# Expert up projections: half of the contraction on fp32r operands in two parts, the other half in plain fp32

## The chip, the cores and the metric

The kernel runs on one core of a Trainium2 chip. The metric is the device time of one execution in microseconds (us): the median of three timed runs. A profile of one further execution shows what each engine did: TensorE (PE, with PEld for its weight loads), VectorE (DVE), ScalarE (ACT), GpSimd (POOL) and SyncE (SP, here only a DMA queue).

## The reference

The program is a two-layer backbone. Each layer normalizes and modulates 512 latent tokens and 256 context tokens of width 1024, mixes them by attention and a gated delta rule, and then runs a mixture of 32 experts. The second layer gives no context output, so its experts see the latent tokens only. The change lies in the experts:

```python
def expert_block(args):
    xi, e = args
    return (jax.nn.silu(xi @ w1[e]) * (xi @ w3[e])) @ w2[e]

y = lax.map(expert_block, (xb, blk_e)).reshape(P, D)
return jax.ops.segment_sum(y[dest] * w_s[:, None].astype(y.dtype), tok_s, num_segments=N)
```

Each token goes to two experts. `w1` and `w3` of an expert are 1024x256 (the up projections), `w2` is 256x1024 (the down projection), all fp32: 1 MB each, 3 MB per expert, 32 experts, two layers.

## The kernel before

One block of up to 128 tokens belongs to each expert. `experts` (L1408) walks over the 32 experts of a layer in a loop that is software pipelined over three experts. In the pass of expert e it

- issues the loads of expert e + 3 (`load`, on SP's queue; `w13` holds w1 and w3 in four buffers, `w2` in three, constants `RB, RB2`),
- multiplies the turned token block `xt` with `w13` into the PSUM tile `pab`, in two groups of four 128-row slices (`expert_up`, L1351), and between the two groups turns the product `u` of expert e - 1 (`expert_turn`: two transposes into `gt`, ScalarE's copy `gh`, VectorE's rest `gl`) and scatters the output of expert e - 2 (`ey` on VectorE, L1400, then a scatter-add `yd` by an indirect DMA from GpSimd's queue, L1405),
- splits `w2` of expert e into two parts (`split`: ScalarE writes `w2h`, L1329, in the type fp32r, VectorE the rest `w2l` = `w2` - `w2h`, L1330),
- makes the gate rows `eg` (`row_gates`: ScalarE, and in layer 0, where latent and context tokens have gates of their own, VectorE too, L1381),
- turns the gathered tokens `xe` of expert e + 1 (`expert_rows`: eight transposes in two groups, each copied by ScalarE to `xt`, L1345),
- computes `u` = silu times the other half (`expert_mid`: ScalarE's tanh and two VectorE instructions, all named `eu`),
- multiplies the turned `u` of expert e - 1 with its `w2` (`expert_down`: twelve products into `py`, L1393), and fetches the tokens of expert e + 4 (gather `xe`, L1334).

In plain fp32 a product appears as two records of TensorE; the down projection uses three fp32r products for each slice, `gh` x `w2h`, `gl` x `w2h` and `gh` x `w2l`, one record each. The order on each engine is that of the program: `pin` (L162) ties each instruction of the stage to the one before it on its engine. The DMAs on SP's queue are not pinned; a scheduler orders them. Each queue issues in order, so a DMA that waits for its buffer holds up those behind it. In some early experts the loop also takes a step of `route_rest`, small instructions on all engines that place overflowing tokens.

Of the kernel before, what the change touches and what calls it, by code (L numbers as in the profile page):

```python
# [13 lines left out]
F32 = mybir.dt.float32  # L14
F32R = mybir.dt.float32r
BF16 = mybir.dt.bfloat16
I32 = mybir.dt.int32
AF = mybir.ActivationFunctionType
OP = mybir.AluOpType
# [4 lines left out]
P = 128  # L24
# [6 lines left out]
NE = 32  # L31
# [63 lines left out]

NOV = 12
NC = NE + NOV
RB, RB2 = 4, 3
YL = 1
XI = 2  # L100
WH = 3
# [42 lines left out]
class Model:  # L144
# [17 lines left out]
    def pin(self, ins):  # L162

        if self.pinned:
            e = ins.ins.engine.name
            if self.last.get(e):
                self.tc.add_manual_dep(ins.ins, self.last[e], mybir.DependencyInfo(mybir.DependencyClass.NoSync, mybir.DependencyReason.DATA), reason="order")
            self.last[e] = ins.ins.name
        return ins
# [1152 lines left out]
        nc.sync.dma_start(dst, src.rearrange("(p k) f -> p k f", **dims))  # L1322
        return w

    def split(self, src, pool, eng):
        nc = self.nc
        hi = pool.tile([P, 2048], F32R, tag="w2h", bufs=2, name="w2h")
        lo = pool.tile([P, 2048], F32R, tag="w2l", bufs=2, name="w2l")
        self.pin(nc.scalar.activation(hi, src, AF.Copy))  # L1329
        self.pin(eng.tensor_tensor(lo, src, hi, op=OP.subtract))  # L1330
        return hi, lo

    def gather(self, idx, xe, h2d, ntok):
# [3 lines left out]
    def expert_rows(self, xe, pool):  # L1337

        nc, pin = self.nc, self.pin
        xt = pool.tile([P, 8, P], F32, tag="xt", bufs=2, name="xt")  # L1340
        for q in range(2):
            ps = self.psC("xt")
            for k in range(4):
                pin(nc.tensor.transpose(ps[:, k * P:(k + 1) * P], xe.rearrange("p (q k) -> p k q", k=8)[:, 4 * q + k, :], self.ident))  # L1344
            pin(nc.scalar.activation(xt[:, 4 * q:4 * q + 4, :], ps.rearrange("p (k n) -> p k n", k=4), AF.Copy))  # L1345
        return xt

    def expert_up(self, pa, xt, w13, ks):

        for k in ks:  # L1350
            self.pin(self.nc.tensor.matmul(pa.rearrange("p (a f) -> p a f", a=2), xt[:, k, :], w13[:, :, k, :], start=(k == 0), stop=(k == 7)))  # L1351

    def expert_mid(self, pa, pool):

# [53 lines left out]
    def experts(self, i, R, js, g5, h2d, yd, ntok, xw):  # L1408


        nc, tc = self.nc, self.tc
        idx, wt = R["idx"], [R[nm] for nm in ("wsl", "wc") if nm in R]
        col = lambda c: idx[:, c:c + 1]
        w13, raw2, w2, x, u, g, gates, py = {}, {}, {}, {}, {}, {}, {}, {}

        def load(e):
            if e < NE:
                for n in range(2):
                    w13[e] = self.expert_load(i, e, n, xw)
                raw2[e] = self.expert_load(i, e, 2, xw)  # L1420

        def fetch(e):
            if e < NE:
                self.gather(col(e), xes[e % XE], h2d, ntok)

        def rows(e):
            if e < NE:
                x[e] = self.expert_rows(xes[e % XE], xp)

        def turn(e):  # L1430
            if e >= 0:
                g[e] = self.expert_turn(u.pop(e), xp)

        def down(e):
            if e >= 0:
                py[e] = self.expert_down(g.pop(e), w2.pop(e))

        def out(e):
            if e >= 0:
                y = self.expert_out(py.pop(e), gates.pop(e), xp)  # L1440
                self.expert_add(y, col(e), yd, ntok)

        self.pins(False)
        for n in range(2):
            w13[0] = self.expert_load(i, 0, n, xw)
        stored = yield
        with tc.issue_after(stored.ins):
            raw2[0] = self.expert_load(i, 0, 2, xw)
            for e in range(1, LA):
                load(e)  # L1450
        xp = yield
        rest = self.route_rest(R, js, xp)
        eo, nb = R["eo"], R["nb"]
        xes = []
        self.pins(True)
        for e in range(XE):
            xes.append(xp.tile([P, D], F32, name="xe%d" % e, tag="xe%d" % e))
            self.pin(nc.gpsimd.memset(xes[e], 0.0))
            fetch(e)
        rows(0)  # L1460
        for e in range(NE):
            load(e + LA)
            pa = self.psA("pab")
            xt, w = x.pop(e), w13.pop(e)
            self.expert_up(pa, xt, w, range(0, 4))
            turn(e - 1)
            out(e - 2)
            self.expert_up(pa, xt, w, range(4, 8))
            w2[e] = self.split(raw2.pop(e), xw, nc.vector)
            gates[e] = self.row_gates([w[:, e:e + 1] for w in wt], g5, xp)  # L1470
            rows(e + 1)
            u[e] = self.expert_mid(pa, xp)
            down(e - 1)
            fetch(e + XE)
            if e >= E0:
                next(rest, None)
        turn(NE - 1)
        out(NE - 2)
        down(NE - 1)
        out(NE - 1)  # L1480
        self.pins(False)
        assert not list(rest)
        n = nc.values_load(nb[0:1, 0:1], min_val=0, max_val=NOV)  # L1483
        with tc.If(n > 0):
            with tc.For_i(0, n, 1) as j:
                ev = nc.values_load(eo[0:1, bass.ds(j, 1)], min_val=0, max_val=NE - 1)
                ic = xp.tile([P, 1], I32, tag="ic", name="ic")
                wo = [xp.tile([P, 1], F32, tag="wo%d" % z, name="wo") for z in range(len(wt))]
                nc.vector.tensor_copy(ic, idx[:, bass.ds(NE + j, 1)])
                for a, w in zip(wo, wt):  # L1490
                    nc.vector.tensor_copy(a, w[:, bass.ds(NE + j, 1)])
                ws = [self.expert_load(i, ev, n, xw) for n in range(3)]
                self.gather(ic, xes[0], h2d, ntok)
                xr = self.expert_rows(xes[0], xp)
                pa = self.psA("pab")
                self.expert_up(pa, xr, ws[0], range(8))
                po = self.expert_down(self.expert_turn(self.expert_mid(pa, xp), xp), self.split(ws[2], xw, nc.vector))
                self.expert_add(self.expert_out(po, self.row_gates(wo, g5, xp), xp), ic, yd, ntok)
        yield

# [268 lines left out]
```

## Time and profile before

| | us |
|---|---|
| median of three timed runs | 2114.71 (2108.64 to 2114.74) |
| profiled execution | 2130.51 |
| its span in the profile | 2128.7 |
| TensorE busy (share of the span) | 1824.3 (86%) |
| VectorE busy | 1272.6 (60%) |
| ScalarE busy | 893.5 (42%) |
| GpSimd busy | 839.5 (39%) |
| fp32 records of the up projection, L1351 | 465.5 |

The profiled execution is one run, 15.8 us over the median of the others. The experts of layer 0 run from about 753 to 1096 us of the span, those of layer 1 from about 1753 to 2095. Busy time of TensorE is pipelined, so its records overlap; the distance between starts tells its pace.

### The profile page before, as it was taken

To read this page: it belongs to the slowest core of one execution; us is meant where nothing else is said; L and a number is where in the kernel's file an instruction comes from. 1 tells how busy PE (TensorE), PEld (TensorE's weight loads), DVE (VectorE), ACT (ScalarE), POOL (GpSimd) and SP (SyncE) were. 2 spreads that over 40 slices of the span, in tenths; PEclk is the share of its full clock that TensorE was granted. 3 is DMA by queue.
4 is the path that set the end of the run, shared out by engine and by line. 5 is a ranking of instruction groups with operands and counts; after the bars stand their busy time and mean duration, and the time that the engine had idled before them with its cause. 6 is when DMAs were issued, how large, how long until landed. Compare 5 with 4: busy or idle time off the path is not lost. (4 is left out here: it accounts for less than half of the span.)

```text
span 2128.7 us, 34974 instructions
## 1 busy us (share of the span) xinstructions
PE 1824.3 (86%) x13579; PEld 1349.2 (63%) x13579; DVE 1272.6 (60%) x2344; ACT 893.5 (42%) x1531; POOL 839.5 (39%) x915
## 2 busy tenths in 40 slices
PE   6998798888868789999978987767888769999995
PEld 4887687666657655565547876656566555566553
DVE  3469996566672645555546689963676443444443
ACT  3444245655541134444425543334464223444442
POOL 4456653244354323223326376520333632223221
PEclk9999897798988889999998988766998779999997
DMA  8222435787655588889924224356862568888872
GB/s 278 72 71 79 127 117 175 233 230 237 199 135 131 198 329 329 323 320 328 331 65 140 80 71 120 107 170 182 252 186 70 174 265 307 326 315 302 314 263 85
DMA packets 227684, 427.77 MB, mean 201 GB/s; under 512 B 83720, under 2 KB 157180, under 8 KB 202939
## 3 DMA queue, kind: packets, MB, share of 16 engines
q1 hardware_dynamic: 171547, 329.09, 45.9%
q0 software_dynamic: 33536, 72.59, 12.1%
q10 hardware_dynamic: 22432, 23.81, 3.3%
q8 instruction: 109, 1.79, 0.3%
q14 instruction: 60, 0.49, 0.1%
HBM read 386.82 MB, written 84.67 MB: 221 GB/s over the span
## 5 line engine op out<-in xcount | busy, mean ns | idle before, releaser
L1351 PE MATMUL pab<-w,xt 128*128 128x512 f32 x1024 | 465.5, 598 | 0.5 <-ACT xt L1345 0.5
L1351 PEld LDWEIGHTS pab<-w,xt 128*128 128x128 f32 x1024 | 189.7, 192 | 191.3 <-issue 186.5
L1405 POOL DMA_INDIRECT yd<-ey,idx x64 | 116.8, 1824 | 472.3 <-DMA yd<-ey,idx 196.9
L1372 DVE TENSOR_TENSOR gl<-gt,gh 128x256 fp32r<-128x256 f32 x64 | 27.1, 424 | 276.1 <-ACT gh L1371 272.5
L1330 DVE TENSOR_TENSOR w2l<-w,w2h 128x2048 fp32r<-128x2048 f32 x64 | 147.4, 2303 | 44.4 <-ACT w2h L1329 43.0
L1371 ACT ACTIVATE gh<-gt 128x256 fp32r<-128x256 f32 x64 | 24.5, 383 | 348.9 <-PE gt L1367 348.9
L238 PE MATMUL pn<-whi,hh 128*128 128x256 f32 (+1 forms) x432 | 133.9, 313 | 15.3 <-ACT gev L1541 11.4
L488 POOL TENSOR_TENSOR wlo<-wraw,whi 128x1024 fp32r<-128x1024 f32 (+1 forms) x44 | 112.0, 2547 | 82.8 <-ACT whi L487 81.9
L238 PE MATMUL po<-woh,m 128*128 128x512 f32 x320 | 113.0, 431 | 27.8 <-ACT woh L1068 20.6
L238 PE MATMUL pn<-whi,hl 128*128 128x256 f32 (+1 forms) x432 | 133.4, 313 | 0.7 <-DVE hl L349 0.4
L238 PE MATMUL pn<-wlo,hh 128*128 128x256 f32 (+1 forms) x432 | 133.0, 309 | 0.6 <-POOL wlo L488 0.6
L238 PE MATMUL pt<-hh,wlo 128*128 128x512 f32 (+1 forms) x352 | 125.4, 356 | 0.0
L238 PE MATMUL pt<-hh,whi 128*128 128x512 f32 (+1 forms) x352 | 124.3, 353 | 0.0
L238 PE MATMUL pt<-hl,whi 128*128 128x512 f32 (+1 forms) x352 | 123.8, 352 | 0.0
L1329 ACT ACTIVATE w2h<-w 128x2048 fp32r<-128x2048 f32 x64 | 121.7, 1902 | 0.0
L1393 PE MATMUL py<-w2h,gh 128*128 128x512 f32 x256 | 107.7, 421 | 4.4 <-DVE ey L1400 4.4
L1345 ACT ACTIVATE xt<-xt 128x512 f32<-128x512 f32 x128 | 69.7, 595 | 86.8 <-PE xt L1344 86.0
L517 DVE SCALAR_TENSOR_TENSOR dT<-xin,cw,dT 128x772 f32<-128x772 f32 x64 | 79.4, 1243 | 42.2 <-ACT dT L515 40.5
L238 PEld LDWEIGHTS pn<-whi,hh 128*128 128x128 f32 x432 | 90.1, 210 | 20.8 <-ACT gev L1541 12.1
L1393 PE MATMUL py<-w2l,gh 128*128 128x512 f32 x256 | 101.6, 397 | 0.0
L1393 PE MATMUL py<-w2h,gl 128*128 128x512 f32 x256 | 101.2, 395 | 0.0
L1344 PEld LDWEIGHTS xt<-cst,xe 128*128 128x128 f32 x512 | 67.9, 192 | 50.2 <-issue 29.8
(391 smaller groups left out, 4561.8 us busy)
## 6 DMA issues: line engine op xcount, KB each, us to landing
w<-w SPq DMA_DIRECT2D x192, 1024.0 KB, 10.0
araw<-ada_w POOLq DMA_DIRECT2D x40, 1024.0 KB, 9.3
wraw<-w_in SPq DMA_DIRECT2D x40, 512.0 KB, 4.1
lk<-vk SPq DMA_DIRECT2D x48, 256.0 KB, 7.2
lx<-xad SPq DMA_DIRECT2D x40, 256.0 KB, 9.3
araw<-ada_w SPq DMA_DIRECT2D x8, 1024.0 KB, 11.8
wr<-w_out SPq DMA_DIRECT2D x8, 1024.0 KB, 15.4
vk<-vr ACTq DMA_DIRECT2D x16, 384.0 KB, 3.2
```

The costliest lines, as they stand in the source:

```text
L238: self.nc.tensor.matmul(ps, a(k), b(k), start=(first and n == 0), stop=(last and n == 3 * nk - 1))
L488: getattr(nc, eng).tensor_tensor(lo, raw, hi, op=OP.subtract)
L517: nc.vector.scalar_tensor_tensor(dst, xin[:, tap:tap + 772], cw[:, tap, f:f + 1], dst, op0=OP.mult, op1=OP.add)
L1329: self.pin(nc.scalar.activation(hi, src, AF.Copy))
L1330: self.pin(eng.tensor_tensor(lo, src, hi, op=OP.subtract))
L1344: pin(nc.tensor.transpose(ps[:, k * P:(k + 1) * P], xe.rearrange("p (q k) -> p k q", k=8)[:, 4 * q + k, :], self.ident))
L1345: pin(nc.scalar.activation(xt[:, 4 * q:4 * q + 4, :], ps.rearrange("p (k n) -> p k n", k=4), AF.Copy))
L1351: self.pin(self.nc.tensor.matmul(pa.rearrange("p (a f) -> p a f", a=2), xt[:, k, :], w13[:, :, k, :], start=(k == 0), stop=(k == 7)))
L1371: pin(nc.scalar.activation(gh, p3, AF.Copy))
L1372: pin(nc.vector.tensor_tensor(gl, p3, gh, op=OP.subtract))
L1393: pin(self.nc.tensor.matmul(py[:, n * 512:(n + 1) * 512], a[:, j, :], b[:, c], start=(j + m == 0), stop=(j == 1 and m == 2)))
L1405: self.pin(self.nc.gpsimd.indirect_dma_start(out=yd, out_offset=bass.IndirectOffsetOnAxis(ap=idx, axis=0), in_=y, in_offset=None, bounds_c ...
```

## The change

The first half of the contraction (four of the eight 128-row slices, constant `KS`) is computed from operands in two parts: three fp32r products in place of one fp32 product. For this `expert_rows` copies the first four turned slices as `xth` (ScalarE) and `xtl` (VectorE, from PSUM minus `xth`), and a new step `parts` splits the first half of `w13` into `w13h` (ScalarE) and `w13l` (VectorE), through the same `split`. The parts of `w13` have one buffer each, those of `w2` two as before. `parts` of expert e + 1 stands in the loop after the second group of `expert_up` and before the split of `w2`. The other half of the contraction stays in fp32. The raw `w2` goes from three buffers to two. The block for overflowing tokens gets the same split.

```diff
-RB, RB2 = 4, 3
+RB, RB2 = 4, 2
+KS = 4
...
-    def split(self, src, pool, eng):
-        nc = self.nc
-        hi = pool.tile([P, 2048], F32R, tag="w2h", bufs=2, name="w2h")
-        lo = pool.tile([P, 2048], F32R, tag="w2l", bufs=2, name="w2l")
+    def split(self, src, name, pool):
+
+        nc = self.nc
+        hi, lo = [pool.tile([P, 2048], F32R, tag="s" + name + z, bufs=2 if name == "w2" else 1, name=name + z) for z in "hl"]
+        if len(src.shape) == 4:
+            hi, lo = [a.rearrange("p (a k f) -> p a k f", a=2, k=KS) for a in (hi, lo)]
         self.pin(nc.scalar.activation(hi, src, AF.Copy))
-        self.pin(eng.tensor_tensor(lo, src, hi, op=OP.subtract))
+        self.pin(nc.vector.tensor_tensor(lo, src, hi, op=OP.subtract))
...
-        xt = pool.tile([P, 8, P], F32, tag="xt", bufs=2, name="xt")
+        xh, xl = [pool.tile([P, KS, P], F32R, tag=nm, bufs=2, name=nm) for nm in ("xth", "xtl")]
+        xt = pool.tile([P, 8 - KS, P], F32, tag="xt", bufs=2, name="xt")
...
-            pin(nc.scalar.activation(xt[:, 4 * q:4 * q + 4, :], ps.rearrange("p (k n) -> p k n", k=4), AF.Copy))
-        return xt
-
-    def expert_up(self, pa, xt, w13, ks):
-
-        for k in ks:
-            self.pin(self.nc.tensor.matmul(pa.rearrange("p (a f) -> p a f", a=2), xt[:, k, :], w13[:, :, k, :], start=(k == 0), stop=(k == 7)))
+            p3 = ps.rearrange("p (k n) -> p k n", k=4)
+            pin(nc.scalar.activation(xt if q else xh, p3, AF.Copy))
+            if q == 0:
+                pin(nc.vector.tensor_tensor(xl, p3, xh, op=OP.subtract))
+        return xh, xl, xt
+
+    def expert_up(self, pa, x, w13, hi_lo, half):
+
+        (xh, xl, xt), (hi, lo) = x, hi_lo
+        out = pa.rearrange("p (a f) -> p a f", a=2)
+        for k in range(4):
+            if half == 0:
+                for m, (a, b) in enumerate(((xh, hi), (xl, hi), (xh, lo))):
+                    self.pin(self.nc.tensor.matmul(out, a[:, k, :], b[:, :, k, :], start=(k + m == 0), stop=False))
+            else:
+                self.pin(self.nc.tensor.matmul(out, xt[:, k, :], w13[:, :, KS + k, :], start=False, stop=(k == 3)))
...
+        def parts(e):
+            if e < NE:
+                p13[e] = self.split(w13[e][:, :, 0:KS, :], "w13", xw)
...
+        parts(0)
         rows(0)
...
-            self.expert_up(pa, xt, w, range(0, 4))
+            self.expert_up(pa, xt, w, hl, 0)
             turn(e - 1)
             out(e - 2)
-            self.expert_up(pa, xt, w, range(4, 8))
-            w2[e] = self.split(raw2.pop(e), xw, nc.vector)
+            self.expert_up(pa, xt, w, hl, 1)
+            parts(e + 1)
+            w2[e] = self.split(raw2.pop(e), "w2", xw)
```

On VectorE, one pass of the loop in layer 0 reads before the change (`w_...` is a raw weight buffer, `eg` the gate row):

```order
L1372 TENSOR_TENSOR gl<-gt,gh 128x256 [waits Activation_49]
L1400 TENSOR_TENSOR ey<-py,eg 128x1024 [waits DMASW4_49]
L1330 TENSOR_TENSOR w2l<-w_8191,w2h 128x2048 [waits DMAHW5_49,Activation_49]
L1381 SCALAR_TENSOR_TENSOR eg<-g_7326,wc,eg 128x1024 [waits Activation_49]
L1358 SCALAR_TENSOR_TENSOR eu<-eu,pab 128x256 [waits PE_49,Activation_49]
L1359 SCALAR_TENSOR_TENSOR eu<-eu,pab 128x256 [waits DVE_49]
```

and after it:

```order
L1385 TENSOR_TENSOR gl<-gt,gh 128x256 [waits Activation_49]
L1413 TENSOR_TENSOR ey<-py,eg 128x1024 [waits DMASW4_49]
L1333 TENSOR_TENSOR w13l<-w_8315,w13h 128x2048 [waits DMAHW3_49,DMAHW2_49,Activation_49]
L1333 TENSOR_TENSOR w2l<-w_8228,w2h 128x2048 [waits DMAHW7_49,Activation_49]
L1394 SCALAR_TENSOR_TENSOR eg<-g_7326,wc,eg 128x1024 [waits Activation_49]
L1352 TENSOR_TENSOR xtl<-xt,xth 128x512 [waits Activation_49]
L1371 SCALAR_TENSOR_TENSOR eu<-eu,pab 128x256 [waits Activation_49]
L1372 SCALAR_TENSOR_TENSOR eu<-eu,pab 128x256 [waits DVE_49]
```

The split of the next expert's up weights stands ahead of that of `w2`, and `xtl` behind both and behind the gate.

On TensorE, the end of one down projection, the first group of the next expert and the turn read after the change (before it, the group was four products `pab<-w,xt` in a row):

```order
L1406 MATMUL py<-w2l,gh 128x512
L1362 MATMUL pab<-w13h,xth 128x512 [waits Activation_49]
L1362 MATMUL pab<-w13h,xtl 128x512 [waits DVE_49]
L1362 MATMUL pab<-w13l,xth 128x512
L1362 MATMUL pab<-w13h,xth 128x512
```

The second product of the group waits for VectorE, and `gt` still follows the group.

On SP's queue, where a name that comes twice in a row is a pair w1 and w3 and a single one is `w2`, the early loads of layer 0 read before the change

```order
L1322 DMA w_8127<-w 128x2048 [waits DMAHW6_49,PE_49]
L1322 DMA w_8127<-w 128x2048 [waits DMAHW7_49]
L1322 DMA w_8188<-w 128x2048 [waits DMAHW0_49,PE_49]
L1322 DMA w_8188<-w 128x2048 [waits DMAHW1_49]
L1322 DMA w_8130<-w 128x2048 [waits DMAHW2_49,DVE_49]
```

and after it

```order
L1323 DMA w_8225<-w 128x2048 [waits DMAHW7_49,PE_49]
L1323 DMA w_8225<-w 128x2048 [waits DMAHW0_49]
L1323 DMA w_8096<-w 128x2048 [waits DMAHW1_49,DVE_49]
L1323 DMA w_8315<-w 128x2048 [waits DMAHW2_49,PE_49]
L1323 DMA w_8315<-w 128x2048 [waits DMAHW3_49]
L1323 DMA w_8152<-w 128x2048 [waits DMAHW6_49,DMAHW4_49,DVE_49]
```

Before, `w_8130` (of expert 4) follows the pair of expert 5; after, `w_8096` (of expert 3) follows it: the load of `w2` stands one expert later against the pairs, and waits for the split that ends the use of its buffer.

## Rows read from the trace of the kernel before

**Rows 1.** Windows: stretch, length, busy us of engines (instructions), granted clock, DMA share, GB/s.

```profile
752.00:774.00 22.00, 21.76 (x68) 11.90 (x67) 9.00 (x9) 9.97 (x13) 1.98 (x2) 0.90 0.84 322
774.00:850.00 76.00, 76.00 (x268) 45.18 (x267) 42.73 (x50) 32.21 (x42) 24.34 (x25) 1.00 0.85 321
```

**Rows 2.** Timeline, TensorE, one expert: start, length, instruction, count [idle before, releaser].

```profile
827.66 3.60 PE L1351 MATMUL pab<-w,xt 128*128 128x512 f32 x8
831.09 0.39 PE L1367 MATMUL gt<-cst,eu 128*128 128x128 f32 x2
...
835.88 0.39 PE L1393 MATMUL py<-w2h,gl 128*128 128x512 f32 x1
...
838.44 3.60 PE L1351 MATMUL pab<-w,xt 128*128 128x512 f32 x8
841.88 0.39 PE L1367 MATMUL gt<-cst,eu 128*128 128x128 f32 x2
```

**Rows 3.** Timeline, VectorE, the same expert of layer 0.

```profile
831.99 0.42 DVE L1372 TENSOR_TENSOR gl<-gt,gh 128x256 fp32r<-128x256 f32 x1 [4.61 <-ACT gh L1371]
832.33 1.21 DVE L1400 TENSOR_TENSOR ey<-py,eg 128x1024 f32<-128x1024 f32 x1
833.79 2.29 DVE L1330 TENSOR_TENSOR w2l<-w,w2h 128x2048 fp32r<-128x2048 f32 x1 [0.25 <-ACT w2h L1329]
836.00 1.28 DVE L1381 SCALAR_TENSOR_TENSOR eg<-g,wc,eg 128x1024 f32<-128x1024 f32 x1
837.20 0.41 DVE L1358 SCALAR_TENSOR_TENSOR eu<-eu,pab 128x256 f32<-128x256 f32 x1
837.64 0.42 DVE L1359 SCALAR_TENSOR_TENSOR eu<-eu,pab 128x256 f32<-128x256 f32 x1
```

**Rows 4.** Timeline, ScalarE, the same expert.

```profile
831.85 1.90 ACT L1329 ACTIVATE w2h<-w 128x2048 fp32r<-128x2048 f32 x1
833.65 1.14 ACT L1379 ACTIVATE eg<-g,wsl 128x1024 f32<-128x1024 f32 x1
```

**Rows 5.** Timeline, TensorE and VectorE, one expert of layer 1.

```profile
1906.84 0.39 PE L1367 MATMUL gt<-cst,eu 128*128 128x128 f32 x2
...
1909.54 2.29 DVE L1330 TENSOR_TENSOR w2l<-w,w2h 128x2048 fp32r<-128x2048 f32 x1 [0.24 <-ACT w2h L1329]
1912.59 0.42 DVE L1358 SCALAR_TENSOR_TENSOR eu<-eu,pab 128x256 f32<-128x256 f32 x1 [0.76 <-ACT eu L1357]
```

**Rows 6.** Timeline, TensorE: first expert, first and last `gt` of both layers.

```profile
752.80 8.91 PE L1351 MATMUL pab<-w,xt 128*128 128x512 f32 x16
762.83 3.70 PE L1351 MATMUL pab<-w,xt 128*128 128x512 f32 x8 [0.24 <-ACT xt L1345]
766.37 0.39 PE L1367 MATMUL gt<-cst,eu 128*128 128x128 f32 x2
...
1092.68 0.39 PE L1367 MATMUL gt<-cst,eu 128*128 128x128 f32 x2
...
1766.68 0.39 PE L1367 MATMUL gt<-cst,eu 128*128 128x128 f32 x2
...
2091.08 0.39 PE L1367 MATMUL gt<-cst,eu 128*128 128x128 f32 x2
```

**Rows 7.** The tile `w` in layer 0's experts: its loads.

```profile
DMA to landing us min/median/max: 6.0/11.8/18.3
```

**Rows 8.** Timeline, GpSimd and VectorE: scatter-adds beside a split.

```profile
950.15 1.63 POOL L1405 DMA_INDIRECT yd<-ey,idx  x1 [7.54 <-DMA yd<-ey,idx]
...
1953.32 2.29 DVE L1330 TENSOR_TENSOR w2l<-w,w2h 128x2048 fp32r<-128x2048 f32 x1 [0.24 <-ACT w2h L1329]
1954.51 2.62 POOL L1405 DMA_INDIRECT yd<-ey,idx  x1 [6.25 <-DMA yd<-ey,idx]
...
1987.91 2.02 POOL L1405 DMA_INDIRECT yd<-ey,idx  x1 [7.09 <-DMA yd<-ey,idx]
1998.22 2.41 POOL L1405 DMA_INDIRECT yd<-ey,idx  x1 [6.94 <-DMA yd<-ey,idx]
```

More of the change, by code (lines that the diff above doesn't have):

```diff
@@ L1413, in experts @@
         col = lambda c: idx[:, c:c + 1]
-        w13, raw2, w2, x, u, g, gates, py = {}, {}, {}, {}, {}, {}, {}, {}
+        w13, p13, raw2, w2, x, u, g, gates, py = {}, {}, {}, {}, {}, {}, {}, {}, {}
         def load(e):
@@ L1463, in experts @@
             pa = self.psA("pab")
-            xt, w = x.pop(e), w13.pop(e)
-            self.expert_up(pa, xt, w, range(0, 4))
+            xt, w, hl = x.pop(e), w13.pop(e), p13.pop(e)
+            self.expert_up(pa, xt, w, hl, 0)
             turn(e - 1)
             out(e - 2)
-            self.expert_up(pa, xt, w, range(4, 8))
-            w2[e] = self.split(raw2.pop(e), xw, nc.vector)
+            self.expert_up(pa, xt, w, hl, 1)
+            parts(e + 1)
+            w2[e] = self.split(raw2.pop(e), "w2", xw)
             gates[e] = self.row_gates([w[:, e:e + 1] for w in wt], g5, xp)
@@ L1495, in experts @@
                 pa = self.psA("pab")
-                self.expert_up(pa, xr, ws[0], range(8))
-                po = self.expert_down(self.expert_turn(self.expert_mid(pa, xp), xp), self.split(ws[2], xw, nc.vector))
+                hl = self.split(ws[0][:, :, 0:KS, :], "w13", xw)
+                for half in range(2):
+                    self.expert_up(pa, xr, ws[0], hl, half)
+                po = self.expert_down(self.expert_turn(self.expert_mid(pa, xp), xp), self.split(ws[2], "w2", xw))
                 self.expert_add(self.expert_out(po, self.row_gates(wo, g5, xp), xp), ic, yd, ntok)
```

## The prediction

> **What bounds the kernel now.** I read the windows of the two expert stages first, then the timeline of one expert, engine by engine, then the waits of the queues. The windows show TensorE busy in 76.00 of 76.00 us, at the full granted clock, while VectorE is busy in 42.73 [rows 1]. So the stage lasts as long as TensorE's own work for an expert. I count a period from one first turn-back transpose (`gt`, called G below) to the next: 831.09 to 841.88 is 10.79 us, without a gap on TensorE [rows 2]. Over a whole layer it is 1092.68 - 766.37 = 326.31 us for 30 periods in layer 0 and 2091.08 - 1766.68 = 324.40 us in layer 1, 10.88 and 10.81 each [rows 6]; the extra is the small routing products between some experts.
>
> VectorE has a hole in each period. Its row of 831.99 carries 4.61 us of idle time that ended with ScalarE's `gh`: it could not go on before TensorE had turned `u` [rows 3]. This hole can't be filled at will, since what stands behind `gl` in its queue waits with it. That matters more here than its share of busy time.
>
> **The change, part by part.**
>
> *TensorE.* Four plain fp32 products of an expert, 831.09 - 827.66 = 3.43 us [rows 2], become twelve on operands in two parts. The down projection `py` has such products in the same shape: eleven steps from 835.88 to 838.44 are 2.56 us, 0.233 each [rows 2]. Twelve are 2.80. TensorE's own work per expert falls from 10.79 to 10.16.
>
> *ScalarE* gains one 128x2048 copy, 1.90, as `w2h` [rows 4]. It is busy 32.21 of 76 us now [rows 1], 4.6 of a period; 6.5 is still far under 10. It has room; the question is what waits for it.
>
> *VectorE* gains `w13l`, which is `w2l` in shape, and `xtl`. `w2l` holds the engine for 836.00 - 833.79 = 2.21 us [rows 3]. `xtl` is not in the trace; it reads PSUM and SBUF, as `gl` (256 elements, 0.42) and `ey` (1024, 1.21) do, which bound it on both sides; along the line between them 512 elements are 0.69 [rows 3].
>
> Now the order. In VectorE's queue `xtl` of the next expert stands behind `w13l`, `w2l` and, in layer 0, the second gate `eg`; and the second of the twelve products needs `xtl`. `gl` in turn waits for a transpose that TensorE issues behind those twelve. So the change closes a ring, and each link has its row. From G:
> - to the first split on VectorE: 833.79 - 831.09 = 2.70 [rows 2, 3]. `w2l` stands there now, released by `w2h` after 0.25 of idle time; `w13l` and `w13h` take the same places. In layer 1 it is 1909.54 - 1906.84 = 2.70 too [rows 5].
> - `w13l` 2.21, then `w2l` 2.21.
> - `eg`, layer 0 alone: 837.20 - 836.00 = 1.20 [rows 3]. Layer 1 has none: after `w2l` VectorE idles 0.76 until `eu` [rows 5].
> - `xtl` 0.69.
> - TensorE takes it up: 0.05, and 0.10 as its next group runs 3.70 in place of 3.60 after a wait of 0.24 for the first expert's `xt` [rows 2, 6]. The ends are 0.05 and 0.24.
> - the eleven products that are left: 2.56; then the next G.
>
> Layer 0: 2.70 + 2.21 + 2.21 + 1.20 + 0.69 + 0.15 + 2.56 = 11.72. Layer 1: 10.52. Both exceed TensorE's 10.16, so the ring and not TensorE sets the pace, and the 0.63 saved there turns into waiting: 1.56 us per expert in layer 0 and 0.36 in layer 1.
>
> What I cost at nothing: the second `xt` copy, `eu` and the gates on ScalarE lie beside the splits; the two `eu` of VectorE, 837.64 - 837.20 + 0.42 = 0.86 [rows 3], and the small routing pieces follow `xtl` and lie in the 0.15 + 2.56 + 0.90 us until the next `gl`, which leaves 2.75 unused; without that cover each us there would be a us of the ring.
>
> The first expert. TensorE's first sixteen records took 8.91 us instead of 7.03 [rows 6] (twice the 3.43 of a group of eight, and the tail of the last one), so some 3.8 us at 1.2 of its 2.4 GHz; the window that holds it has a granted clock of 0.90 [rows 1]. With `xtl` 0.69 after the start (753.5), about six and a half of the eleven products run at twice 0.233 and the group ends near 757.6. One buffer for the parts means that `w13h` of expert 1 waits for this: 0.1 + 1.90 + 2.21 + 2.21 + 1.20 + 0.69 + 0.15 + 2.56 leads to G at 768.6 against 766.37, +2.3. Layer 1, without the gate, +1.1.
>
> Sum. Layer 0: 30 x 11.72 = 351.6 against 326.3, +25.3, and +2.3. Layer 1: 30 x 10.52 = 315.6 against 324.4, -8.8, and +1.1. Together +19.9 us. The profiled execution took 2130.51 us (span 2128.7, 1.8 around it), so its like would be 2150.4; the timed runs have a median of 2114.71, 15.8 less, and I take the difference over to them: **2134.6 us**.
>
> *The loads.* `w2` has two buffers, so load k+2 is issued when `w2l` of k ends, one expert later than now. From G + 2.70 + 2.21 + 2.29 to its use at G + 2.56 two periods on (ScalarE's second copy, 0.76 after G plus 1.80 [rows 2, 4]) are 2P - 4.64: 18.8 us in layer 0, 16.4 in layer 1. Loads land in 11.8 us at the median, 18.3 at the longest [rows 7]. Costed at nothing. The up weights are needed an expert sooner for their split, but are issued at the end of `pab` four experts ahead as before.
>
> **The rivals.**
>
> *TensorE stays the bound; faster.* If `w13l` ran in VectorE's hole ahead of `gl`, the ring would lose 2.21 and TensorE's 10.16 would decide: 30 x 10.16 = 304.8, so -21.5 and -19.6, with +3.4 of the first experts -37.7, 2077 us. For it: the hole is there (4.61). Against it: the queue order, and the one buffer, which holds `w13h` of the next expert back until the twelve products have read the last one, so the hole ends before the split may start. The point from which it decides: the mean of the two periods must come below (326.3 + 324.4 - 3.4)/60 = 10.79; mine is 11.12. A miss of 0.33 us per period would turn the sign; `eg` alone, outside the ring in layer 0, would do it (2134.6 - 30 x 1.20 = 2098.6).
>
> *The scatter chain.* Each `yd` scatter-add waits for the one before: 1987.91 and 1998.22 are 10.31 apart, the second after 6.94 us that the DMA ended [rows 8]. It keeps pace today. But GpSimd's issue at 1954.51 came in the midst of `w2l` (1953.32 to 1955.61) and took 2.62 where another takes 1.63; it ended 1.5 after `w2l` did [rows 8]. Splits will stand there for 4.4 us in a row in layer 1, 5.6 with the gate in layer 0. If a landing comes at any point of a period, the mean delay is half the square of that stretch over the period, 0.9 and 1.3 us: 11.2 in layer 1, over its 10.52, and 11.6 in layer 0, just under its 11.72. The lag grows by 0.7 per expert until an `ey` buffer, wanted two experts later, is not free. An issue at G + 7.1 lands at 17.4; `ey` wants it at 2 x 10.52 + 1.24 = 22.3 [rows 2, 3], so 4.9 us are free and 30 x 0.7 - 4.9 = 16 are paid: 2151 us. Against it: an issue held until the splits end lands about 10.3 later, shortly before the next splits end, and so falls in step with the ring.
> [...]
>
> *`w2` comes late.* If every load took the longest landing, 18.3 us, the two buffers would set (18.3 + 4.64)/2 = 11.47 in layer 1, +0.95 x 30: 2163 us. For it: it is the buffer count that sets this lead, and it falls by a whole expert. Against it: median 11.8, DMA share 0.85 [rows 1, 7].
>
> **How the numbers follow.** Forecast 0.66, its own range 2120 to 2148 (0.24 us of pick-up in place of 0.15, `xtl` from 0.42 to 1.21, that is -0.27 to +0.52 per period, 60 periods, not all at once); scatter chain 0.16; late `w2` 0.07; TensorE the bound or nearly, 0.11. A measurement of this kernel tells about 0.3%, 6.3 us, from no change. Faster by more than that holds most of the last case, 0.08; within it the rest and the low end of the forecast, 0.08; slower 0.84. The range leaves out the fast case and half of the late loads: 2112 to 2160.
>
> **What would show it.** Right: periods of about 11.7 and 10.5 us between `gt` rows; TensorE waiting in front of `pab<-w13h,xtl`, released by VectorE's `xtl`; VectorE's queue without idle time from `w13l` to `xtl`; ScalarE with waits left. Wrong: periods of 10.2 with TensorE full; `ey` waiting for the scatter's DMA; `w2h` or `w13h` waiting for a load; a granted clock under 1.00 in the stage.

## The result and the profile after

The changed kernel took 2146.51 us (median of four, 2143.33 to 2152.49) beside 2114.72 for the kernel before (four, 2108.64 to 2119.57): a ratio of 1.0149, 95% interval 1.0120 to 1.0178. Timed again in the experiments it took 2140.17 beside 2115.14, ratio 1.0109 (1.0086 to 1.0133). I had predicted 2134.6, range 2112 to 2160, which is 19.9 us over the kernel before; the two sets measured 31.8 and 25.0. The sign, the place and the ring were right. The expert stages came out at the predicted sum, in part by errors that cancel; about 5.7 us more lie outside them, in a place that I had not priced.

Windows of the changed kernel (stretch, length, busy us of TensorE, its weight loads, VectorE, ScalarE and GpSimd, granted clock, DMA share, GB/s): two of layer 0, one of layer 1. These rows and the next are of its first profile, span 2142.2.

```profile
788.00:864.00 76.00, 66.81 (x272) 45.71 (x271) 57.37 (x62) 37.82 (x43) 32.02 (x24) 1.00 0.83 306
864.00:1115.00 251.00, 225.65 (x923) 154.52 (x923) 193.99 (x217) 135.87 (x151) 87.51 (x55) 1.00 0.80 285
1800.00:2100.00 300.00, 298.24 (x1223) 205.21 (x1223) 219.43 (x239) 180.86 (x201) 96.30 (x77) 1.00 0.85 309
```

TensorE was busy in all of its 76 us [rows 1]; now it is idle in 9.2 of 76 in layer 0, and in next to nothing of layer 1, where its short waits vanish in the overlap of its records. VectorE, which sets the pace, is busy in 57.37 of 76: a queue can bind at three quarters of its time.

TensorE over one expert of layer 0 (start, length, instruction, count, idle time before and its releaser), to be read against [rows 2]:

```profile
781.49 0.39 PE L1380 MATMUL gt<-cst,eu 128*128 128x128 f32 x2
781.72 3.60 PE L1364 MATMUL pab<-w,xt 128*128 128x512 f32 x8
...
788.84 0.39 PE L1362 MATMUL pab<-w13h,xth 128*128 128x512 f32 x1
790.55 0.50 PE L1362 MATMUL pab<-w13h,xtl 128*128 128x512 f32 x1 [1.32 <-DVE xtl L1352]
...
793.23 0.39 PE L1380 MATMUL gt<-cst,eu 128*128 128x128 f32 x2
```

VectorE in the same expert, against [rows 3]:

```profile
782.33 0.42 DVE L1385 TENSOR_TENSOR gl<-gt,gh 128x256 fp32r<-128x256 f32 x1 [2.78 <-ACT gh L1384]
...
784.13 2.37 DVE L1333 TENSOR_TENSOR w13l<-w,w13h 128x2048 fp32r<-128x2048 f32 x1 [0.24 <-ACT w13h L1332]
786.42 2.28 DVE L1333 TENSOR_TENSOR w2l<-w,w2h 128x2048 fp32r<-128x2048 f32 x1
788.62 1.27 DVE L1394 SCALAR_TENSOR_TENSOR eg<-g,wc,eg 128x1024 f32<-128x1024 f32 x1
789.82 0.68 DVE L1352 TENSOR_TENSOR xtl<-xt,xth 128x512 fp32r<-128x512 f32 x1
```

The ring closes in 793.23 - 781.49 = 11.74 us. Link by link: 784.13 - 781.49 = 2.64 to `w13l` (predicted 2.70), `w13l` 2.29 (2.21), `w2l` 2.20 (2.21), `eg` 1.20 (1.20), `xtl` and its pick-up 790.55 - 789.82 = 0.73 and then 2.68 to the next `gt` (together 3.41; predicted 0.69 + 0.15 + 2.56 = 3.40). From `w13l` to `xtl` VectorE has no idle time. Layer 1, VectorE, against [rows 5]:

```profile
1919.28 2.41 DVE L1333 TENSOR_TENSOR w13l<-w,w13h 128x2048 fp32r<-128x2048 f32 x1 [0.24 <-ACT w13h L1332]
1921.62 2.28 DVE L1333 TENSOR_TENSOR w2l<-w,w2h 128x2048 fp32r<-128x2048 f32 x1
1923.82 0.68 DVE L1352 TENSOR_TENSOR xtl<-xt,xth 128x512 fp32r<-128x512 f32 x1
...
1929.84 2.29 DVE L1333 TENSOR_TENSOR w13l<-w,w13h 128x2048 fp32r<-128x2048 f32 x1 [0.24 <-ACT w13h L1332]
```

Here `xtl` stands right behind `w2l`, and one turn is 1929.84 - 1919.28 = 10.56; the mean period of the layer is 10.46. The waits between 780 and 1110 us (who waits, for whom, us in all, times, longest) name the same link, and neither of the two slower rivals: `ey` and `w2h` wait for no DMA.

```profile
PEld pab L1362 <- DVE xtl L1352: 45.2, 28, 2.5
PE pab L1362 <- DVE xtl L1352: 34.5, 28, 2.1
```

In layer 1 (waits, 1800 to 2100 us) it is the weight loads that show it; no load or scatter stands there either:

```profile
PEld pab L1362 <- DVE xtl L1352: 10.5, 21, 0.7
```

Where the time went, from the two profiles that were taken together (the kernel before, span 2115.2, and the changed one, 2142.9). A stage runs from the first `xt` transpose of a layer to its 31st `gt`:

| | before | changed | difference |
|---|---|---|---|
| layer 0: first `xt` to first `gt` | 15.69 | 19.03 | +3.3 |
| layer 0: 30 periods | 30 x 10.877 | 30 x 11.742 | +26.0 |
| layer 1: first `xt` to first `gt` | 15.34 | 16.83 | +1.5 |
| layer 1: 30 periods | 30 x 10.814 | 30 x 10.454 | -10.8 |
| last logits to first `xt`, layer 0 | 20.06 | 23.47 | +3.4 |
| last logits to first `xt`, layer 1 | 20.14 | 22.43 | +2.3 |
| all the rest of the span | 1393.3 | 1395.3 | +2.0 |

The stages give +20.0, the routing +5.7, together 25.7; the timed medians of that set lie 25.0 apart.

### The profile page after: what moved, and what is told of

The parts are those of the page before. It is cut to its first block, busy times and chain, and to the rows that moved or that the text cites. A ratio compares the mean times of both kernels' runs of the same rounds, so it can differ in the third digit from the quotient of the medians.

```text
span 2142.2 us, 35513 instructions
## 1 busy us (share of the span) xinstructions
PE 1794.9 (84%) x13835; PEld 1391.3 (65%) x13835; DVE 1453.0 (68%) x2472; ACT 1004.2 (47%) x1595; POOL 871.8 (41%) x915
## 3 DMA queue, kind: packets, MB, share of 16 engines
q0 software_dynamic: 33536, 72.59, 11.8%
## 5 line engine op out<-in xcount | busy, mean ns | idle before, releaser
L1418 POOL DMA_INDIRECT yd<-ey,idx x64 | 121.5, 1898 | 456.0 <-DVE ey L1413 194.3
L1364 PE MATMUL pab<-w,xt 128*128 128x512 f32 x512 | 230.5, 593 | 0.0
L1333 DVE TENSOR_TENSOR w13l<-w,w13h 128x2048 fp32r<-128x2048 f32 x64 | 148.4, 2319 | 30.9 <-ACT w13h L1332 30.9
L1364 PEld LDWEIGHTS pab<-w,xt 128*128 128x128 f32 x512 | 93.2, 192 | 92.0 <-issue 91.8
L1362 PE MATMUL pab<-w13h,xtl 128*128 128x512 f32 x256 | 109.5, 428 | 42.7 <-DVE xtl L1352 41.1
L1332 ACT ACTIVATE w13h<-w 128x2048 fp32r<-128x2048 f32 x64 | 121.8, 1902 | 12.7 <-PE pab L1362 8.6
L1362 PE MATMUL pab<-w13h,xth 128*128 128x512 f32 x256 | 104.8, 409 | 1.6 <-ACT xth L1350 1.6
```

Source lines behind the costliest of these rows:

```text
L1333: self.pin(nc.vector.tensor_tensor(lo, src, hi, op=OP.subtract))
L1362: self.pin(self.nc.tensor.matmul(out, a[:, k, :], b[:, :, k, :], start=(k + m == 0), stop=False))
L1364: self.pin(self.nc.tensor.matmul(out, xt[:, k, :], w13[:, :, KS + k, :], start=False, stop=(k == 3)))
L1418: self.pin(self.nc.gpsimd.indirect_dma_start(out=yd, out_offset=bass.IndirectOffsetOnAxis(ap=idx, axis=0), in_=y, in_offset=None, bounds_c ...
```

## The experiments

Edits are against the changed kernel unless another is named.

**Both kernels again**, as they are.

> The kernel before once more, for a second profile of it. Its first profiled execution was 15.8 us over its timed median, and the two profiles differ by 13.5 us of span while the timed runs differ by 31.8. Theory A (the ring alone): the stretch from the first token transpose to the last turn of the experts lasts 341.7 us in layer 0 and 339.7 in layer 1 again, within 1 us; what was slow in the first profile lies outside the experts, in the stretch between the two expert stages (658.7 us then, about 645 now). Rival B (the change also slows the mixer of layer 1): that stretch stays near 652 to 659 and the time near 2115 can't be found in it.

> The changed kernel once more. Theory A: the stretches of the experts last 371.5 and 330.6 us within 1 us, +20.7 against before, and what is left of the timed difference (31.8) is spread of the rest of the program from run to run, so the stretch between the stages differs from the first profile's 652.1 by several us. Rival B: that stretch is 652 again and some 10 us longer than in the kernel before.

Measured: 2113.33, ratio 0.9987 (0.9969 to 1.0005), and 2140.17, ratio 1.0109 (1.0086 to 1.0133). The table above is theirs. The profile of the kernel before that my sum started from had a span 13.5 us longer; its stages differ from these by under 0.5 us, so none of that lay in the experts. It did not lie between the stages either, where I had expected it: 10.2 of the 13.5 us lie ahead of the last logits of layer 0 (730.7 and 720.5 us from the start), in the same kernel.

**The second gate out of the ring.**

```diff
...
             w2[e] = self.split(raw2.pop(e), "w2", xw)
-            gates[e] = self.row_gates([w[:, e:e + 1] for w in wt], g5, xp)
             rows(e + 1)
             u[e] = self.expert_mid(pa, xp)
+            gates[e] = self.row_gates([w[:, e:e + 1] for w in wt], g5, xp)
```

> The changed kernel with the gate rows made behind the tanh product of the same pass: VectorE's second gate instruction (1.20 us, layer 0 alone) leaves the stretch between the split of w2 and xtl. Work is the same on every engine. Ring theory: the period of layer 0 falls from 11.75 to 10.55, layer 1 stays at 10.46; 31 x 1.20 = 37 us less, 2109 us. Rival (VectorE's load or its blocking of GpSimd sets the pace, not the order): no change, 2146. Rival (scatter chain is next): layer 0 stops at about 10.9 or above, 2120.

Measured: 2107.38, ratio 0.9971 (0.9951 to 0.9992). VectorE in layer 0 (timeline):

```profile
798.87 2.28 DVE L1333 TENSOR_TENSOR w2l<-w,w2h 128x2048 fp32r<-128x2048 f32 x1
801.07 0.68 DVE L1352 TENSOR_TENSOR xtl<-xt,xth 128x512 fp32r<-128x512 f32 x1
...
802.45 1.28 DVE L1394 SCALAR_TENSOR_TENSOR eg<-g,wc,eg 128x1024 f32<-128x1024 f32 x1
```

With `eg` behind `eu` the first twelve periods are 10.46 to 10.55, layer 1's pace: the ring without its 1.20. So one instruction of an engine that is off the critical path by its share of busy time turned 1.1% slower into 0.3% faster. Then the periods go to 10.7 to 12.4, 11.3 on the mean, so that the stage of layer 0 falls by 25.7 us (371.30 to 345.58) and not by the 37 that I had expected; the timed 32.8 lie in part outside the stages. Between 920 and 1090 us the waits show a new one: the loads of `w2`.

```profile
PEld pab L1362 <- DVE xtl L1352: 16.5, 16, 2.3
ACT w2h L1332 <- DMA w<-w: 15.6, 14, 2.2
```

**The products with `xtl` last**, so that TensorE has eight products to do before it needs `xtl`.

```diff
...
-                for m, (a, b) in enumerate(((xh, hi), (xl, hi), (xh, lo))):
...
+            for m, (a, b) in enumerate(((xh, hi), (xh, lo), (xl, hi))):
+                for k in range(4):
...
```

> The changed kernel with the twelve products in another order: xth x w13h for the four slices, then xth x w13l, then xtl x w13h. xtl is wanted eight products later, and the ring loses 7 x 0.233 = 1.63 us. Ring theory: layer 0 would be 10.1 and layer 1 8.8 by the ring, so TensorE's 10.16 decides in both: -48 -9 -3 us, about 2087, faster than before. Rival (loads and scatters are next: 3.5 MB an expert in 10.16 us would be about 350 GB/s, over the 321 to 333 seen so far): periods of 10.4 to 10.8, VectorE's ey or ScalarE's copies waiting for a DMA, 2095 to 2115.

Measured: 2104.84, ratio 0.9949 (0.9932 to 0.9965). TensorE's `gt` rows in layer 0:

```profile
826.87 0.39 PE L1381 MATMUL gt<-cst,eu 128*128 128x128 f32 x2
837.02 0.39 PE L1381 MATMUL gt<-cst,eu 128*128 128x128 f32 x2
...
888.88 0.39 PE L1381 MATMUL gt<-cst,eu 128*128 128x128 f32 x2
900.11 0.39 PE L1381 MATMUL gt<-cst,eu 128*128 128x128 f32 x2
```

The first two are 10.15 apart: TensorE alone, the 10.16 that I had worked out for it. In layer 1 19 of the 30 periods are 10.03 to 10.07, where the changed kernel has 10.43: the ring was the limit there too. In layer 0 the periods are 11.2 on the mean from about 880 us on. The windows before and after that point, and a row of ScalarE:

```profile
790.00:864.00 74.00, 74.00 (x313) 52.55 (x312) 64.45 (x62) 46.82 (x54) 28.24 (x26) 1.00 0.91 332
885.00:1080.00 195.00, 185.32 (x754) 125.99 (x754) 157.39 (x176) 109.54 (x123) 72.79 (x47) 1.00 0.86 305
```

```profile
993.26 1.91 ACT L1332 ACTIVATE w2h<-w 128x2048 fp32r<-128x2048 f32 x1 [1.22 <-DMA w<-w]
```

The loads issued between 885 and 1080 us take 4.9/18.0/20.1 us (shortest, median, longest); in the second profile of the changed kernel 4.7/8.6/12.2 (the first has landings for few of them). My lead for those of `w2` was 2P - 4.64, which is 17.8 at this pace. The landings grew all through the fast periods, from 11.3 for those issued at 785 to 815 us to 18.4 at 875 to 905 us, and the pace fell when they had used up the lead. `w2h` then waits for its load, and `w2l` and `xtl` stand behind it in VectorE's queue, so this limit reaches TensorE over the same link. So the rival in which `w2` comes late holds once the ring is open, in layer 0; no run shows it at the ring's pace.

**Two buffers for `w2` in the kernel before**, nothing else (`RB2 = 2` for 3).

> The kernel before with one part of the change alone: w2 in two buffers in place of three. Theory (the loss of the change is VectorE's ring, the buffer count costs nothing at periods of 10.8 and more): 341.9 us and 339.7 us for the two expert stretches again, 2115 within 4. Rival (the two buffers cost part of the 25 us): w2h waiting for loads, 5 us or more over the kernel before.

Measured: 2117.56, ratio 1.0012 (0.9997 to 1.0027), stages 342.01 and 339.74 against 342.00 and 339.75. The lost buffer costs nothing by itself.

**`w2l` behind `xtl` and `eu`** on VectorE, and the gates behind it (with `True`, `split` leaves out its subtraction).

```diff
...
-            w2[e] = self.split(raw2.pop(e), "w2", xw)
-            gates[e] = self.row_gates([w[:, e:e + 1] for w in wt], g5, xp)
+            r2 = raw2.pop(e)
+            w2[e] = self.split(r2, "w2", xw, True)
             rows(e + 1)
             u[e] = self.expert_mid(pa, xp)
+            self.pin(nc.vector.tensor_tensor(w2[e][1], r2, w2[e][0], op=OP.subtract))
+            gates[e] = self.row_gates([w[:, e:e + 1] for w in wt], g5, xp)
```

> The changed kernel with VectorE's work in another order: w13l, xtl, the two eu, then w2l and the gate (ScalarE: w13h, w2h, xth, xt, eu, gate). xtl comes 3.4 us sooner, so the ring is under TensorE's 10.16 in both layers; the w2 buffer is freed later (at about G + 9), which leaves its load 2P - 6.5 = 13.8 us instead of 15.7. Theory R (loads and scatters of layer 0 cannot be moved faster than one expert in about 11.1 us): the first ten periods 10.16, then about 11.2 as in the run with xtl last, 2105. Theory L (the lead of the two w2 buffers decides): with a landing of 18 us the period of layer 0 rises to (18 + 6.5)/2 = 12.2, 2130. Ring theory alone: 10.16 throughout, 2085.

Measured: 2103.94, ratio 0.9944 (0.9921 to 0.9966), stages 339.64 and 323.59. The ring is gone, and two waits stand in its place between 885 and 1080 us:

```profile
ACT w2h L1332 <- DMA w<-w: 29.0, 13, 3.2
DVE ey L1414 <- DMA yd<-ey,idx: 22.8, 14, 3.9
```

**The same with three `w2` buffers**, paid for with a single buffer for `w2l`.

> The same order of VectorE with three w2 buffers (paid with one buffer for w2l). The load of w2 has 3P - 6.5 = 24 us. Theory R: layer 0 still goes to about 11.1 after some 12 periods, since the queue is what is full; w2h or TensorE waits for some load; about 2103. Theory L: no wait for w2 any more, 10.2 throughout layer 0, 2090 or less.

Measured: 2110.40, ratio 0.9984 (0.9967 to 1.0001), stages 338.90 and 323.64. The profiled execution took 2102.0. Neither of my two theories held: no wait of `w2h` for a load is left, yet layer 0 slows down all the same, and the other wait has grown. Waits from 885 to 1080 us, and two rows of GpSimd:

```profile
DVE ey L1414 <- DMA yd<-ey,idx: 33.2, 17, 4.3
```

```profile
961.24 1.63 POOL L1419 DMA_INDIRECT yd<-ey,idx  x1 [7.53 <-DMA yd<-ey,idx]
972.47 1.64 POOL L1419 DMA_INDIRECT yd<-ey,idx  x1 [6.95 <-DMA yd<-ey,idx]
```

972.47 - 961.24 = 11.23: the chain of scatter-adds, one behind the other, now sets the period. The issues take 1.63 here; it is the transfers that are slow, not the issue that my rival had priced: from issue to landing 10.4 us at the median between 885 and 1080 us, and 4.7 to 6.1 for the last five of the layer, issued when its loads had landed.

**Three `ey` buffers**, so that the scatters may lag: once on the kernel with `xtl` last, once on the last one (both with a single buffer for `xth` and `xtl`; `tag="ey", bufs=2` becomes 3), and the latter also with the small `rrsl` of the overflow routing made by VectorE.

> The run with xtl last, with three ey buffers (paid with one buffer each for xth and xtl). In that run ey waited 12 us for scatter-adds in layer 1, in periods of up to 13.3. Scatter theory: ey never waits, the long periods of layer 1 go, its mean falls from 10.35 to 10.1, 8 us less; layer 0 as it was; 2097. Rival (the long periods come from the routing pieces behind GpSimd's scatters, not from the buffer): layer 1 keeps periods over 11, 2105.

> VectorE's order of the run with w2l behind xtl, three w2 buffers and three ey buffers together. Scatter theory (with w2 early enough, ey's wait for the scatter-add is what holds layer 0 after the twelfth period): no wait of w2h for a load, hardly one of ey; what is left are the routing products that wait for GpSimd's rrsl, which stands behind the scatters; stretches of about 335 and 320 us, 2097. Rival (loads as such cannot come faster): layer 0 keeps a mean period near 10.7 to 10.8 with waits for loads, 2100 to 2104.

> The same, with the routing piece rrsl made by VectorE in place of GpSimd, so that TensorE's routing product no longer waits behind a scatter-add. Scatter theory: periods 10.16 and 10.4 (with the routing product) nearly throughout, stretches of about 326 to 330 and 318 us, 2090. Rival (loads): as the run before it, with w13h, w2h or TensorE waiting for loads.

Measured: 2099.75, ratio 0.9928 (0.9902 to 0.9953), stages 336.37 and 319.88; 2112.03, ratio 0.9967 (0.9945 to 0.9990), 337.50 and 323.59; 2105.15, ratio 0.9942 (0.9919 to 0.9964), 330.74 and 320.60. The last two are 15 us slower than I had expected. In the first, `ey` waits for no scatter any more and the mean period of layer 1 falls from 10.35 to 10.19; the interval of its time overlaps that of the kernel without the third buffer. In the second, `ey` waits for none either, but TensorE stands before a routing product for a small GpSimd instruction, in a queue that the scatters hold (waits, 920 to 1090 us):

```profile
PEld rest L1302 <- POOL rrsl L1297: 6.6, 2, 3.3
```

In the third that is gone, and the gathers, which share GpSimd's queue with the scatters, come late (waits, 885 to 1080 us):

```profile
PEld xt L1349 <- DMA xe<-h2d,idx: 10.3, 7, 1.9
```

Its stages are 30.4 us shorter than before's, its time only 11.3. That sent me to look outside the stages. In the two profiles 6.1 us of it are the routing, dealt with next; 8.0 lie ahead of the last logits of layer 0, where two profiles of the same kernel differ as much, and no run shows a cause for them.

**The first expert's split behind the routing.** The trace of the changed kernel, ScalarE and VectorE just ahead of the experts of layer 0:

```profile
727.20 0.25 DVE L1132 SCALAR_TENSOR_TENSOR lg<-lg,rf,rbs 128x36 f32<-128x36 f32 x1 [0.19 <-PE lg L1128]
729.65 1.91 ACT L1332 ACTIVATE w13h<-w 128x2048 fp32r<-128x2048 f32 x1 [4.03 <-DMA w<-w]
731.47 0.19 ACT L1205 ACTIVATE rtx<-rtx 128x8 f32<-128x8 f32 x1
731.59 2.29 DVE L1333 TENSOR_TENSOR w13l<-w,w13h 128x2048 fp32r<-128x2048 f32 x1 [1.42 <-ACT w13h L1332]
733.80 0.15 DVE L1206 TENSOR_REDUCE rtsg<-rtx 128x2 f32<-128x8 f32 x1
741.51 0.19 DVE L1231 SCALAR_TENSOR_TENSOR idx<-tab,e 128x32 int32<-128x32 f32 x1
```

`w13h` and `w13l` of expert 0 stand in both queues ahead of the last softmax of the routing, and in layer 0 `w13h` held ScalarE's queue for 4.03 us until its load had landed: 14.31 us from the last logits to `idx`, where the kernel before has 741.37 - 730.74 = 10.63:

```profile
730.74 0.25 DVE L1131 SCALAR_TENSOR_TENSOR lg<-lg,rf,rbs 128x36 f32<-128x36 f32 x1 [0.19 <-PE lg L1127]
741.37 0.19 DVE L1230 SCALAR_TENSOR_TENSOR idx<-tab,e 128x32 int32<-128x32 f32 x1
```

The edit was made to the changed kernel, and to the one with `xtl` last and three `ey`:

```diff
...
-        nc.scalar.activation(x8, x8, AF.Exp)
+        R["act"] = nc.scalar.activation(x8, x8, AF.Exp).ins
...
-        parts(0)
+        with tc.issue_after(R["done"]), tc.issue_after(R["act"]): parts(0)
```

> The changed kernel with one edit outside the expert loop: the first expert's w13h and w13l of each layer are queued behind the routing instead of ahead of its last pair. Theory: in the changed kernel the last logits of a layer come 14.3 us (layer 0) and 12.7 us (layer 1) before the first index of the expert table, where the kernel before has 10.6 and 10.5, because ScalarE's copy and VectorE's subtraction of the first expert's weights stand in front of the last softmax of the routing. Queued behind, both distances fall to 10.6 and 10.5, the split runs beside the gathers (9.1 to 9.9 us), and the time falls by 5.0 to 6.0 us against the changed kernel, 2135 to 2139 where that had 2140 and 2146. The expert stages keep their 371 and 330 us. Rival A: the routing's distance is covered by something else, the first transposes of the experts come no earlier and the time stays at 2140 to 2146. Rival B: the split now ends after the first rows are turned, and TensorE waits for w13l in front of the first products by 1 to 3 us, which gives half of it back.

> The best kernel so far (the products with xtl last, three ey buffers) with the same edit: the first expert's split queued behind the routing. Theory: 3.6 and 2.2 us less from the last logits to the first index, the stages as they were (336.4 and 319.9 us), so 2093 to 2096 us after 2099.75, a ratio to the kernel before of 0.990. Rival A: nothing changes, 2098 to 2101, ratio 0.993. Rival B: the split comes late for the first expert's products with w13l and half is given back, 2096 to 2098.

Measured: 2137.20, ratio 1.0102 (1.0075 to 1.0130); and 2103.16, ratio 0.9945 (0.9921 to 0.9970). In both, logits to `idx` fell to 10.6 or 10.7 in layer 0 and 10.5 in layer 1, as the theory said. But from `idx` to the first `xt` it now takes 10.4 and 11.0 us instead of 9.2 and 9.8. The changed kernel with the edit, VectorE and GpSimd:

```profile
739.87 2.28 DVE L1333 TENSOR_TENSOR w13l<-w,w13h 128x2048 fp32r<-128x2048 f32 x1
740.72 2.49 POOL L1337 DMA_INDIRECT xe<-h2d,idx  x1 [7.93 <-DMA w<-w]
```

The first gather's issue took 2.49 beside the split; without it 1.18:

```profile
742.56 1.18 POOL L1337 DMA_INDIRECT xe<-h2d,idx  x1 [11.58 <-DVE wsl L1244]
```

So rival B was right that part is given back, and wrong about how. Net, last logits to first `xt` went from 23.47 and 22.43 to 21.04 and 21.46: 3.4 of the 5.7 us, and the medians of the two sets differ by 3.0. The intervals overlap, so the timing alone does not show it; the rows do. (Its stage of layer 0 is also 2.0 shorter, 369.30, which I had not expected.) On the faster kernel the same gain in the routing did not show in the time: 2103.16 against 2099.75 and an expected 2093 to 2096, intervals overlapping, its profile with stages of 339.22 and 326.11 although the loop is the same. One period of layer 1 alone took 17.5 us there, with TensorE waiting for `rrsl`, the small GpSimd instruction named above; why it came late in this run is not shown. Which of the two is the fastest stays open.

## Why the prediction was right, and where not

**TensorE's own 10.16 and the ring of 11.72 and 10.52: right.** The kernel with `xtl` last ran its first periods at 10.15; the changed kernel at 11.742 and 10.454 on the mean, with `xtl` as the releaser. Each link is within 0.08. Taking `eg` out of the queue ahead of `xtl` gave layer 0 the period of layer 1, for as long as its loads came in time. That the sum for the stages is within 0.1 us (+20.0, predicted +19.9) is luck: the periods of layer 0 came out 0.7 us over the forecast and the first experts 1.4 over, those of layer 1 2.0 under.

**The first expert: mis-sized.** Predicted +2.3 and +1.1, measured +3.3 and +1.5. TensorE, second group of layer 0, and the windows there:

```profile
765.71 0.50 PE L1362 MATMUL pab<-w13h,xtl 128*128 128x512 f32 x1 [2.50 <-DVE xtl L1352]
...
767.03 0.63 PE L1362 MATMUL pab<-w13h,xth 128*128 128x512 f32 x1
767.46 0.63 PE L1362 MATMUL pab<-w13h,xtl 128*128 128x512 f32 x1
...
769.60 0.63 PE L1380 MATMUL gt<-cst,eu 128*128 128x128 f32 x2
```

```profile
762.70:766.00 3.30, 0.79 (x2) 0.48 (x3) 3.28 (x4) 0.72 (x2) 2.02 (x1) 1.00 0.94 395
766.00:769.60 3.60, 3.60 (x12) 2.63 (x12) 0.42 (x1) 0.00 (x0) 0.00 (x0) 0.62 0.99 416
```

I had priced the eleven products behind `xtl` at full speed, 2.56. They took 769.60 - 765.71 = 3.89: TensorE had been busy in 0.79 of the 3.30 us before, and the granted clock of the stretch is 0.62, its later steps 0.43 apart, the 1.2 GHz level. In layer 1 the same eleven products took 2.64, the full clock, so the 0.4 there have another cause, which I did not find. I had named a clock under 1.00 as a sign against me, and had looked for it in the steady state only.

**The routing: missed.** What I cost at nothing covered the work beside the splits in the loop; the first split, ahead of the loop, I did not cost at all. It cost 3.4 + 2.3 us. This is about the gap between 2134.6 and 2140.17. The other timed set lies 6.3 higher, at 2146.51; the profiles of both sets have the same stages within 0.3 us and executions of nearly the same time, and no trace says where those 6 us were.

**`w2` late, and the scatter chain: right to leave out, for this pace.** The loads of the changed kernel land in 8.8 us at the median of its second profile (780 to 1110 us), earlier than before (11.8 at the median of [rows 7], 11.9 in the second profile of that kernel). The scatters kept up with the ring: issues of 1.9 us on the mean, and no wait of `ey`. Both became a bound when the ring was opened. So the price that I gave for the gate outside the ring, 2098.6, was too good: it took 1.20 off all 30 periods and left out that the loads of layer 0 would not follow that pace. It measured 2107.38.

**The scatter chain, and GpSimd's issues beside a split.** A split on VectorE, which has two SBUF inputs, lengthened GpSimd's issue: 2.62 for 1.63 [rows 8], and now 2.49 for 1.18 at the gather, ending 1.06 after `w13l` did. But an issue is held by the one split that it meets, and not, as I had priced it, by the whole row of 4.4 or 5.6 us. Two scatter issues of the changed kernel, the first 0.05 behind the start of its `w13l` (949.56), the second with the splits around it:

```profile
949.61 1.64 POOL L1418 DMA_INDIRECT yd<-ey,idx  x1 [6.83 <-DVE ey L1413]
...
984.74 2.29 DVE L1333 TENSOR_TENSOR w13l<-w,w13h 128x2048 fp32r<-128x2048 f32 x1 [0.24 <-ACT w13h L1332]
986.65 1.90 POOL L1418 DMA_INDIRECT yd<-ey,idx  x1 [7.40 <-DMA yd<-ey,idx]
986.95 2.28 DVE L1333 TENSOR_TENSOR w2l<-w,w2h 128x2048 fp32r<-128x2048 f32 x1
```

The second ended at 988.55, 1.52 after `w13l` and well before the end of `w2l`, which started and ran as ever. Of the 64 scatter issues of this profile, 21 began within 0.05 of a split's start; they took 1.54 to 1.64, and the split 2.37 in place of 2.29, which is the 0.08 by which the link of `w13l` is over the forecast (986.95 - 984.74 is the 2.21 that I had priced). The 22 that began later in a split ended 1.44 to 1.53 after it, wherever they had begun; the 21 that met none took 1.54 to 1.66. The Trainium skill, page "SBUF — State Buffer", section "SBUF: two separate sides", says that whichever of the two starts first has the shared ports for its whole instruction, and limits this, for two SBUF inputs, to a GpSimd instruction that reads SBUF. The rows agree for the split, which holds up an issue until it ends; they do not for the issue, beside which a split runs for all but 0.08 us. What of an issue reads SBUF no run shows.

So the rival did not happen: in layer 0 up to 950 us every issue follows `ey`, starts with `w13l` and is not held, and the later ones that are held still leave `ey` without a wait. Where a queue's first transfer waits for a split, outside the loop, it costs its 1.3 us in full.

## What to carry to other kernels

An engine with a quarter of its time idle can set the pace: follow one item through the in-order queues until it comes back to where it started, add the links, and compare with the busiest engine's own sum. What stands in such a queue ahead of the instruction that the busiest engine waits for matters more than how much stands in it; moving one gate of 1.2 us or reordering twelve products undid the whole loss here. And when a pipelined loop gets a new first step, look at where the first iteration's copy of it lands, in the queues of the work ahead of the loop.

## What the runs showed that I had not expected

- Loads of layer 0 that land in 8.6 us at the median in the changed kernel (period 11.74) took 18.0 with `xtl` last (10.15, then 11.2), at nearly the same 306 and 305 GB/s and DMA shares of 0.84 and 0.86 between 885 and 1080 us; in layer 1 of that same kernel they took 8.6 at 311 GB/s. Why layer 0 reaches its limit earlier is not settled.
- Scatter-adds of one block each, in a chain, came 10 to 11 us apart while the loads ran, though their issue takes 1.63 us: this is close to the pace of an expert, so two output buffers are few.
- At the first expert of layer 0, after a stretch of 3.3 us in which it was busy for 0.79, TensorE lost its full clock in the midst of the next group; after the waits of 1.01 to 2.06 us in the later periods it did not (granted clock 1.00 in all three windows of the stages).
